# FFN gate and up tiles as block products of seven multiplications, with one operand summed by an accumulating transfer

## The chip, the cores and the metric

One Trainium2 (trn2) chip, one core. The metric is the device time of one execution of the whole program in microseconds (us), the median of several executions. One more execution is profiled; its trace gives the rows shown below.

## The reference

A decoder trunk of two layers over 512 tokens of width 1024, all in float32. Each layer is a token mixer and then a dense SwiGLU FFN; only the FFN is touched here.

```
FF = 2816
def _swiglu(h, w_gate_up, w_down):
    gu = jnp.einsum('bsd,df->bsf', h, w_gate_up)      # 1024 -> 2 x 2816
    g, u = gu[..., :FF], gu[..., FF:]
    return jnp.einsum('bsf,fd->bsd', jax.nn.silu(g) * u, w_down)
...
    hn = _rmsnorm(h, norm_ffn[layer])
    h = h + _swiglu(hn, w_gate_up[layer], w_down[layer])
```

## The kernel before

The activations lie feature by token: a tile is 128 features on the partitions by T = 512 tokens, and the residual x is KC = 8 such tiles. Float32 products are made of three matmuls: each operand is split into a high part (a copy rounded to fp32r, on ScalarE) and a low part (what the copy lost, a subtraction on VectorE), and `mm3` adds high x high, high x low and low x high in PSUM.

`unit` (L58 to L67) brings 128 x 1024 weights: one load on the SP queue into a buffer of `rawp` (three of them), then `whi` on ScalarE and `wlo` on VectorE (pool `wp`, three of each). `feature_tile` makes one tile of 128 outputs by 512 tokens in a PSUM bank of `psg` (four banks) from such a unit and a list of split inputs. Other tiles lie in two pools of 128 x 512 buffers: `low` (33) and `slots` (39); `slot(name, type, low)` picks one. Temporary PSUM banks come from `psa` (four).

`ffn` has NF = 22 pairs of tiles. Each pair is one gate tile and one up tile (L549, L554), both over the eight chunks of the input; the input is x times the norm's weight, and the row factor `rb` (the inverse root mean square of each token) is multiplied in afterwards (L551, L555), since the matmuls start before it is known. Silu and the product follow (L552, L556), and the product is split into `a_h` and `a_l`, the first eight pairs into `low`, the others into `slots`. Then each of the eight output tiles is one PSUM bank over all 22 products, loaded in the three pieces of `DOWN`, and is added to x (L564). `feed` prepares the new x tile for the next layer; in the last layer `final_turn` and `finish` do the final norm and the output, and `finish` makes the last tile in two halves of 256 tokens.

No order is written out for the FFN. The engines' queues are filled by a planner, which picks, for each engine, among the instructions whose operands and buffers are there, by their place in the program; each queue then runs in its order, and semaphores hold an instruction until its operands are ready. `tc.keep_in_program_order` and `tc.issue_after` pin single instructions.

Of the kernel before, what the change touches and what calls it, by code (L numbers as in the profile page):

```python
# [16 lines left out]
F32 = mybir.dt.float32  # L17
# [4 lines left out]
ALU = mybir.AluOpType  # L22
# [12 lines left out]
NEG = -1e30  # L35
ORDER = "S0 A0 B0 C0 S1 T0 U0+A1 V0+B1 C1 S2 T1 U1+A2 V1+B2 C2 S3 T2 U2+A3 V2+B3 C3 -0 T3 U3 V3"
WARM = 8
DOWN = [(0, 8), (8, 15), (15, 22)]


class Trunk:
# [196 lines left out]
    def mixer(self, wf, wt, wsb, wro, wout, tabs, dec):  # L238
# [297 lines left out]
        for i in range(8):  # L536
# [3 lines left out]
                self.start_norm(self.norm_col + 1)  # L540
            self.feed(i)

    def ffn(self, wgu, wdn, last):
        nc, xs, slot = self.nc, self.xs, self.slot
        ax = []
        for f in range(NF):
            g = self.feature_tile(wgu[2 * f], xs)
            if f == 0:
                rb = self.rms_rows(self.acc, D)  # L549
            gs = slot("g")  # L550
            nc.vector.tensor_tensor(out=gs, in0=g, in1=rb, op=ALU.mult)  # L551
            nc.scalar.activation(gs, gs, AF.Silu)  # L552
            u = self.feature_tile(wgu[2 * f + 1], xs)
            us = slot("u")  # L554
            nc.vector.tensor_tensor(out=us, in0=u, in1=rb, op=ALU.mult)  # L555
            nc.vector.tensor_tensor(out=us, in0=us, in1=gs, op=ALU.mult)  # L556
            ax.append(self.split(us, "a", f < 8))
        if last:
            self.tc.keep_in_program_order(nc.scalar.preload_act_table_set("sqrt_and_others"))
        for i in range(KC - 1 if last else KC):  # L560
            ps = self.bank()
            for a, b in DOWN:
                self.feature_tile(wdn[i][:, a * P : b * P], ax[a:b], ps, a == 0, b == NF)
            nc.vector.tensor_tensor(out=self.x[i], in0=self.x[i], in1=ps, op=ALU.add)  # L564
            if i == 0:
                self.start_norm(self.norm_col + 1)
            if last:
                self.square(i)
                self.final_turn(i)
            else:  # L570
                self.feed(i)
        return ax


    def final_turn(self, c, lo=0, hi=T):
# [11 lines left out]
            if c == 3:  # L587
                nc.vector.tensor_copy(self.xt[t][0], ps)

    def finish(self, wdn, ax, out):  # L590

        nc, c = self.nc, KC - 1
        units = [self.unit(wdn[c][:, a * P : b * P], (b - a) * P) for a, b in DOWN]
        for lo in (0, T // 2):
            hi = lo + T // 2
            ps = self.bank()[:, : T // 2]
            for (a, b), u in zip(DOWN, units):
                self.feature_tile(u, [(h[:, lo:hi], l[:, lo:hi]) for h, l in ax[a:b]], ps, a == 0, b == NF)
            x = self.x[c][:, lo:hi]
            nc.vector.tensor_tensor(out=x, in0=x, in1=ps, op=ALU.add)  # L600
            sq = self.slot("sq7")
            nc.scalar.activation(sq[:, lo:hi], x, AF.Square)
            self.final_turn(c, lo, hi)
            ts = range(lo // P, hi // P)
            y = self.rms_tokens([self.acc, sq], D, ts)
            for j, t in enumerate(ts):
                xt, rows = self.xt[t], slice(t * P, (t + 1) * P)
                nc.vector.tensor_scalar(out=xt[0], in0=xt[0], scalar1=y[:, j : j + 1], scalar2=None, op0=ALU.mult)
                nc.scalar.activation(xt[1], self.turned[t], AF.Copy, scale=y[:, j : j + 1])
                nc.sync.dma_start(out=out[rows, 0:T], in_=xt[0])  # L610
                nc.scalar.dma_start(out=out[rows, T:D], in_=xt[1])

    def run(self, xT, norms, tabs, dec, sqr, wq, wf, wt, wsb, wro, wout, wgu, wdn, out):
# [15 lines left out]
        nc.gpsimd.affine_select(out=self.keep, in_=self.keep, pattern=[[-1, T]], base=T - P - 1, channel_multiplier=1, compare_op=ALU.not_equal, fill=0.0)  # L629
        for l in range(L):  # L630
            self.mixer(wf[l], wt[l], wsb[l], wro[l], wout[l], tabs, dec)
            ax = self.ffn(wgu[l], wdn[l], l == L - 1)
        self.finish(wdn[L - 1], ax, out)


@with_exitstack
# [65 lines left out]
```

## Time and profile before

| | |
|---|---|
| median of 3 runs | 1655.45 us (1655.44 to 1655.64) |
| the profiled execution's own time | 1655.86 us |
| its span, from the first instruction to the last | 1653.8 us |
| TensorE busy | 1638.4 us (99%) |
| VectorE busy | 952.7 us (58%) |
| ScalarE busy | 689.0 us (42%) |
| GpSimd busy | 69.6 us (4%) |
| moved by DMA | 153.40 MB, 93 GB/s on average |

PE is TensorE's matmuls, PEld its weight loads, DVE VectorE, ACT ScalarE, POOL GpSimd, SP SyncE, whose queue (SPq) issues the loads. L63 is line 63 of the kernel. Busy time of PE is that of pipelined matmuls, whose ends are modelled, so it is their starts that tell the pace.

### The profile page before, as it was taken

What the parts mean: (1) busy time and instruction counts of PE and PEld (TensorE: products, weight loads), DVE (VectorE), ACT (ScalarE), POOL (GpSimd) and SP (SyncE); (2) the same over time, 40 slices, a digit from 0 to 9 for tenths busy, and PEclk for the clock granted to TensorE, in tenths of its full rate; (3) what the DMA queues carried; (4) which work ended last, traced back from release to release, by engine and by line L of the source; (5) the groups of instructions that cost most, each with busy time, mean ns of one, the idle gap of its engine ahead of it and who ended that gap; (6) DMA issues with size and microseconds to landing.
All of it is one profiled execution on the core that took longest, in us unless ns stands there. A gap on an engine that the chain in (4) does not pass through costs nothing.

```text
span 1653.8 us, 18844 instructions
## 1 busy us (share of the span) xinstructions
PE 1638.4 (99%) x7474; PEld 1341.7 (81%) x7474; DVE 952.7 (58%) x1307; ACT 689.0 (42%) x1053; POOL 69.6 (4%) x57
## 2 busy tenths in 40 slices
PE   9999999999999999999999999999999999999998
PEld 7887777888888888888888778888888888888887
DVE  5799878645554444433348987885354544444232
ACT  5667745433342323222227677453324333233222
POOL 2000000000200000001000000000002000000000
PEclk9999999999999999999999999999999999999999
DMA  5322312233333232333332122223333333333331
GB/s 194 103 76 77 102 53 64 89 102 102 95 97 100 92 102 89 97 94 93 101 100 90 64 90 90 62 70 102 98 100 91 103 91 101 94 97 96 92 95 62
DMA packets 45591, 153.40 MB, mean 93 GB/s; under 512 B 5184, under 2 KB 5696, under 8 KB 45504
## 3 DMA queue, kind: packets, MB, share of 16 engines
q1 hardware_dynamic: 43056, 148.00, 29.0%
q10 hardware_dynamic: 2448, 4.22, 0.8%
q8 instruction: 58, 0.95, 0.2%
q14 instruction: 29, 0.24, 0.0%
HBM read 150.10 MB, written 2.10 MB: 92 GB/s over the span
## 4 chain that ended last, share of the span: by engine, by line
PE 89%; DVE 8%; ACT 2%; issue 1%; DMA 0%; SPq 0%; DVEq 0%; ACTq 0%
PE g L80 26%; PE g L79 26%; PE g L81 26%; PE g L111 2%; PE g L112 2%; PE g L113 2%; DVE wlo L65 2%; DVE z L367 1%; PE a L81 1%; DVE rt L295 1%; PE a L80 1%; PE a L79 1%; DVE kl L341 1%; DVE w L363 1%; ACT whi L63 1%
## 5 line engine op out<-in xcount | busy, mean ns | idle before, releaser
L63 ACT ACTIVATE whi<-raw 128x1024 fp32r<-128x1024 f32 (+1 forms) x276 | 289.1, 1048 | 742.5 <-PE g L80 412.1
L80 PE MATMUL g<-xl,whi 128*128 128x512 f32 x1344 | 524.1, 390 | 0.1
L81 PE MATMUL g<-xh,wlo 128*128 128x512 f32 x1344 | 523.5, 389 | 0.0
L79 PE MATMUL g<-xh,whi 128*128 128x512 f32 x1344 | 521.5, 390 | 0.5 <-ACT xh L169 0.5
L65 DVE TENSOR_TENSOR wlo<-raw,whi 128x1024 fp32r<-128x1024 f32 (+1 forms) x276 | 335.9, 1218 | 162.6 <-ACT whi L63 160.6
L79 PEld LDWEIGHTS g<-xh,whi 128*128 128x128 f32 x1344 | 252.3, 188 | 54.0 <-ACT xh L169 1.4
L80 PEld LDWEIGHTS g<-xl,whi 128*128 128x128 f32 x1344 | 252.3, 188 | 52.4 <-DVE xl L171 0.5
L81 PEld LDWEIGHTS g<-xh,wlo 128*128 128x128 f32 x1344 | 252.3, 188 | 52.3
L80 PE MATMUL g<-a_l,whi 128*128 128x512 f32 (+1 forms) x374 | 142.4, 381 | 0.0
L79 PE MATMUL g<-a_h,whi 128*128 128x512 f32 (+1 forms) x374 | 142.2, 380 | 0.0
L81 PE MATMUL g<-a_h,wlo 128*128 128x512 f32 (+1 forms) x374 | 141.7, 379 | 0.0
L555 DVE TENSOR_TENSOR u<-g,rs_y 128x512 f32<-128x512 f32 x44 | 30.4, 691 | 134.8 <-PE g L81 134.8
L228 POOL TENSOR_TENSOR acc<-acc,sq 128x512 f32<-128x512 f32 x34 | 55.7, 1638 | 1069.0 <-ACT sq L227 1068.5
L79 PEld LDWEIGHTS g<-a_h,whi 128*128 128x128 f32 x374 | 70.1, 187 | 14.8
L551 DVE TENSOR_TENSOR g<-g,rs_y 128x512 f32<-128x512 f32 x44 | 30.4, 691 | 89.3 <-PE g L81 89.3
L80 PEld LDWEIGHTS g<-a_l,whi 128*128 128x128 f32 x374 | 70.1, 187 | 14.3
L81 PEld LDWEIGHTS g<-a_h,wlo 128*128 128x128 f32 x374 | 70.1, 187 | 14.2
L111 PE MATMUL g<-whi,xh 128*128 128x512 f32 x192 | 74.9, 392 | 1.0 <-ACT v L314 1.0
L113 PE MATMUL g<-wlo,xh 128*128 128x512 f32 x192 | 75.0, 391 | 0.0
L112 PE MATMUL g<-whi,xl 128*128 128x512 f32 x192 | 74.9, 390 | 0.0
L367 DVE TENSOR_TENSOR_SCAN z<-keep,w 128x256 f32<-128x256 bf16 (+2 forms) x64 | 51.0, 818 | 1.6
L79 PE MATMUL g<-rt_h,whi 128*128 128x512 f32 x128 | 49.8, 389 | 0.0
(162 smaller groups left out, 1927.1 us busy)
## 6 DMA issues: line engine op xcount, KB each, us to landing
raw<-in_wgu SPq DMA_DIRECT2D x88, 512.0 KB, 3.5
raw<-in_wf SPq DMA_DIRECT2D x76, 512.0 KB, 3.5
raw<-in_wdn SPq DMA_DIRECT2D x32, 448.0 KB, 3.3
raw<-in_wt SPq DMA_DIRECT2D x24, 512.0 KB, 3.6
raw<-in_wro SPq DMA_DIRECT2D x16, 512.0 KB, 3.5
raw<-in_wout SPq DMA_DIRECT2D x16, 512.0 KB, 3.6
raw<-in_wdn SPq DMA_DIRECT2D x16, 512.0 KB, 3.6
raw<-in_wsb SPq DMA_DIRECT2D x8, 512.0 KB, 3.5
```

Source lines behind the costliest of these rows:

```text
L63: self.last_hi = nc.scalar.activation(hi[:, :n], raw[:, :n], AF.Copy).ins
L65: nc.vector.tensor_tensor(out=lo[:, :n], in0=raw[:, :n], in1=hi[:, :n], op=ALU.subtract)
L79: mm(out, lhsT=ah, rhs=bh, start=start, stop=False)
L80: mm(out, lhsT=ah, rhs=bl, start=False, stop=False)
L81: self.last_mm = mm(out, lhsT=al, rhs=bh, start=False, stop=stop).ins
L111: mm(out, lhsT=ah, rhs=bh, start=start, stop=False)
L112: mm(out, lhsT=al, rhs=bh, start=False, stop=False)
L113: mm(out, lhsT=ah, rhs=bl, start=False, stop=stop)
L228: nc.gpsimd.tensor_tensor(out=self.acc, in0=self.acc, in1=sq, op=ALU.add)
L367: nc.vector.tensor_tensor_scan(out=s[:, o:e][:, ::-1], data0=keep[:, ::-1], data1=w[:, o:e][:, ::-1], initial=NEG, op0=ALU.mult, op1=ALU.s ...
L551: nc.vector.tensor_tensor(out=gs, in0=g, in1=rb, op=ALU.mult)
L555: nc.vector.tensor_tensor(out=us, in0=u, in1=rb, op=ALU.mult)
```

## The change

Of the 22 pairs of gate and up tiles in a layer, the first five (`PLAIN`) stay as they are; the other 17 are made by `pair`. It sees the pair as a product of a 2 x 2 block matrix of weights (rows: gate and up; columns: the lower and the upper half of the 1024 inputs) with a 2 x 2 block matrix of inputs (rows: the same halves; columns: tokens 0 to 255 and 256 to 511). Seven block products, with sums of blocks as operands, take the place of eight. With A the weights and B the input, S1 = A21 + A22, S2 = S1 - A11, S3 = A11 - A21 and S4 = A12 - S2 are made for each pair, T1 = B12 - B11, T2 = B22 - T1, T3 = B22 - B12 and T4 = T2 - B21 once a layer by `pair_input`, which needs the row factor first, so that the pairs' results aren't multiplied by it afterwards (the code keeps S2, T2 and T4 with the sign turned). Each block product (`block`) is four chunks of three matmuls with 256 tokens.

Sums of products are made in PSUM where matmuls can go on adding in one bank, and by ScalarE copies and VectorE additions elsewhere. S1 is made by two transfers: the first half of the up tile's weights is loaded into a buffer `s1` once more from DRAM, and a transfer issued by GpSimd adds the second half to it. `pair` is a generator with five pieces, and the loop in `ffn` puts the last two pieces of a pair between the first three of the next.

The down projection is cut into two halves of 11 products each. The first is run after pair 12, the second at the end; each adds all eight output tiles into x. The split of a product into its low part (`low_part`) is moved from the pair to the down projection's first tile, whose matmuls are put in an order of their own. `XLOW`, `ALOW` and `LLOW` say which of the new tiles lie in `low`.

```
@@ -35,7 +35,11 @@
 NEG = -1e30
 ORDER = "S0 A0 B0 C0 S1 T0 U0+A1 V0+B1 C1 S2 T1 U1+A2 V1+B2 C2 S3 T2 U2+A3 V2+B3 C3 -0 T3 U3 V3"
 WARM = 8
-DOWN = [(0, 8), (8, 15), (15, 22)]
+PLAIN = 5
+HALF = NF // 2
+XLOW = 8
+ALOW = 16
+LLOW = False
 class Trunk:
@@ -540,10 +544,124 @@
                 self.start_norm(self.norm_col + 1)
             self.feed(i)
+    def raw_unit(self, src):
+        raw = self.rawp.tile([P, 1024], F32, name="raw", tag="raw")
+        self.nc.sync.dma_start(out=raw, in_=src)
+        return raw
+    def pair_weights(self, gate, up):
+        nc, tt = self.nc, self.nc.vector.tensor_tensor
+        a, b = self.raw_unit(gate), self.raw_unit(up)
+        p, q = slice(0, T), slice(T, 2 * T)
+        s1 = self.slot("s1")
+        def wide(src):
+            hi, lo = self.wp.tile([P, 1024], F32R, name="whi", tag="whi"), self.wp.tile([P, 1024], F32R, name="wlo", tag="wlo")
+            nc.scalar.activation(hi, src, AF.Copy)
+            tt(out=lo, in0=src, in1=hi, op=ALU.subtract)
+            return [(hi[:, s], lo[:, s]) for s in (p, q)]
+        w = {}
+        w["A11"], w["A12"] = wide(a)
+        nc.sync.dma_start(out=s1, in_=up[:, p])
+        nc.gpsimd.dma_start(out=s1, in_=up[:, q], accum_op=ALU.add)
+        w["A22"] = self.split(b[:, q], "w")
+        tt(out=b[:, p], in0=a[:, p], in1=b[:, p], op=ALU.subtract)
+        tt(out=b[:, q], in0=a[:, p], in1=s1, op=ALU.subtract)
+        w["S3"], w["S2"] = wide(b)
+        w["S1"] = self.split(s1, "w")
+        tt(out=a[:, q], in0=a[:, q], in1=b[:, q], op=ALU.add)
+        w["S4"] = self.split(a[:, q], "w")
+        return w
+    def pair_input(self, c, rb):
+        nc, tt = self.nc, self.nc.vector.tensor_tensor
+        h = T // 2
+        p, q = slice(0, h), slice(h, T)
+        b1, b2, u, v = (self.slot(n) for n in ("xn", "xn", "xu", "xv"))
+        for t, k in ((b1, c), (b2, c + 4)):
+            nc.vector.scalar_tensor_tensor(out=t, in0=self.x[k], scalar=self.norms[:, self.norm_col * KC + k : self.norm_col * KC + k + 1], in1=rb, op0=ALU.mult, op1=ALU.mult)
+        tt(out=u[:, p], in0=b1[:, q], in1=b1[:, p], op=ALU.subtract)
+        tt(out=u[:, q], in0=b2[:, q], in1=b1[:, q], op=ALU.subtract)
+        tt(out=v[:, p], in0=u[:, p], in1=b2[:, q], op=ALU.subtract)
+        tt(out=v[:, q], in0=b2[:, p], in1=v[:, p], op=ALU.add)
+        low = lambda: self.xlow.pop() if self.xlow else False
+        if c % 2 == 0:
+            l = low()
+            self.b11 = self.slot("xb_h", F32R, l), self.slot("xb_l", F32R, l)
+        s = slice(c % 2 * h, c % 2 * h + h)
+        hi, lo = (t[:, s] for t in self.b11)
+        nc.scalar.activation(hi, b1[:, p], AF.Copy)
+        tt(out=lo, in0=b1[:, p], in1=hi, op=ALU.subtract)
+        self.xf["B11"].append((hi, lo))
+        for t, names in ((b2, ("B21", "B22")), (u, ("T1", "T3")), (v, ("T2", "T4"))):
+            hi, lo = self.split(t, "xf", low())
+            for name, s in zip(names, (p, q)):
+                self.xf[name].append((hi[:, s], lo[:, s]))
+    def block(self, out, w, x, start):
+        hi, lo = w
+        for c, (xh, xl) in enumerate(self.xf[x]):
+            s = slice(c * P, (c + 1) * P)
+            for k, (l, r) in enumerate(((hi, xh), (lo, xh), (hi, xl))):
+                self.nc.tensor.matmul(out, lhsT=l[:, s], rhs=r, start=start and c == 0 and k == 0, stop=c == 3 and k == 2, skip_group_check=True)
+    def pair(self, wgu, f):
+        nc, tt = self.nc, self.nc.vector.tensor_tensor
+        h = T // 2
+        p, q = slice(0, h), slice(h, T)
+        w = self.pair_weights(wgu[2 * f], wgu[2 * f + 1])
+        x, zy = self.bank(), self.abank()
+        t, u3 = self.slot("pu"), self.slot("u3")
+        self.block(x[:, p], w["A11"], "B11", True)
+        nc.scalar.activation(t[:, p], x[:, p], AF.Copy)
+        self.block(zy[:, p], w["A12"], "B21", True)
+        yield
+        self.block(x[:, p], w["S2"], "T2", False)
+        nc.scalar.activation(t[:, q], x[:, p], AF.Copy)
+        self.block(zy[:, q], w["S1"], "T1", True)
+        yield
+        self.block(x[:, p], w["S3"], "T3", False)
+        nc.scalar.activation(u3[:, p], x[:, p], AF.Copy)
+        tt(out=x[:, q], in0=zy[:, q], in1=u3[:, p], op=ALU.add)
+        yield
+        self.block(x[:, p], w["A22"], "T4", False)
+        yield
+        self.block(zy[:, q], w["S4"], "B22", False)
+        tt(out=t, in0=zy, in1=t, op=ALU.add)
+        nc.scalar.activation(t, t, AF.Silu)
+        self.activated(x, t)
+        yield
+    def activated(self, u, g):
+        a, hi = self.slot("a", F32, self.alow()), self.slot("a_h", F32R, self.alow())
+        self.nc.vector.tensor_tensor(out=a, in0=u, in1=g, op=ALU.mult)
+        self.nc.scalar.activation(hi, a, AF.Copy)
+        self.ax.append((hi, a))
+    def alow(self):
+        self.na += 1
+        return (self.na - 1) % (2 * HALF) >= 2 * HALF - ALOW
+    def low_part(self, f):
+        hi, a = self.ax[f]
+        lo = self.slot("a_l", F32R, LLOW)
+        self.nc.vector.tensor_tensor(out=lo, in0=a, in1=hi, op=ALU.subtract)
+        self.ax[f] = hi, lo
     def ffn(self, wgu, wdn, last):
         nc, xs, slot = self.nc, self.xs, self.slot
-        ax = []
-        for f in range(NF):
+        self.ax, self.na, self.xf, self.xlow = [], 0, {n: [] for n in ("B11", "B21", "B22", "T1", "T2", "T3", "T4")}, XLOW * [True]
+        for f in range(PLAIN):
             g = self.feature_tile(wgu[2 * f], xs)
             if f == 0:
                 rb = self.rms_rows(self.acc, D)
@@ -553,15 +671,60 @@
             u = self.feature_tile(wgu[2 * f + 1], xs)
             us = slot("u")
             nc.vector.tensor_tensor(out=us, in0=u, in1=rb, op=ALU.mult)
-            nc.vector.tensor_tensor(out=us, in0=us, in1=gs, op=ALU.mult)
-            ax.append(self.split(us, "a", f < 8))
+            self.activated(us, gs)
+            if f < 4:
+                self.pair_input(f, rb)
+        old = None
+        for f in range(PLAIN, NF):
+            new = self.pair(wgu, f)
+            next(new)
+            if old:
+                next(old)
+            next(new)
+            if old:
+                next(old)
+            next(new)
+            old = new
+            if f == HALF + 1:
+                self.down(wdn, 0, range(KC))
         if last:
             self.tc.keep_in_program_order(nc.scalar.preload_act_table_set("sqrt_and_others"))
-        for i in range(KC - 1 if last else KC):
+        self.down(wdn, 1, range(KC - 1 if last else KC), old, last)
+    def down(self, wdn, half, tiles, old=None, last=False):
+        nc, f0 = self.nc, half * HALF
+        cuts = [(f0, f0 + 6), (f0 + 6, f0 + HALF)]
+        for i in tiles:
             ps = self.bank()
-            for a, b in DOWN:
-                self.feature_tile(wdn[i][:, a * P : b * P], ax[a:b], ps, a == 0, b == NF)
+            units = [(a, b, self.unit(wdn[i][:, a * P : b * P], (b - a) * P)) for a, b in cuts]
+            if i == 0:
+                mm = nc.tensor.matmul
+                for a, b, (hi, lo) in units:
+                    for f in range(a, b):
+                        if old and f == f0 + 4:
+                            next(old)
+                        if old and f == f0 + 6:
+                            next(old)
+                        if f != f0 + HALF - 1 or not old:
+                            self.low_part(f)
+                    for f in range(a, b):
+                        s = slice((f - a) * P, (f - a + 1) * P)
+                        mm(ps, lhsT=hi[:, s], rhs=self.ax[f][0], start=f == f0, stop=False)
+                        mm(ps, lhsT=lo[:, s], rhs=self.ax[f][0], start=False, stop=False)
+                if old:
+                    self.low_part(f0 + HALF - 1)
+                for a, b, (hi, lo) in units:
+                    for f in range(a, b):
+                        s = slice((f - a) * P, (f - a + 1) * P)
+                        mm(ps, lhsT=hi[:, s], rhs=self.ax[f][1], start=False, stop=f == f0 + HALF - 1)
+            else:
+                for a, b, u in units:
+                    self.feature_tile(u, self.ax[a:b], ps, a == f0, b == f0 + HALF)
             nc.vector.tensor_tensor(out=self.x[i], in0=self.x[i], in1=ps, op=ALU.add)
+            if not half:
+                continue
             if i == 0:
                 self.start_norm(self.norm_col + 1)
             if last:
@@ -569,7 +732,6 @@
                 self.final_turn(i)
             else:
                 self.feed(i)
-        return ax
     def final_turn(self, c, lo=0, hi=T):
@@ -587,15 +749,16 @@
             if c == 3:
                 nc.vector.tensor_copy(self.xt[t][0], ps)
-    def finish(self, wdn, ax, out):
+    def finish(self, wdn, out):
         nc, c = self.nc, KC - 1
-        units = [self.unit(wdn[c][:, a * P : b * P], (b - a) * P) for a, b in DOWN]
+        cuts = [(HALF, HALF + 6), (HALF + 6, NF)]
+        units = [self.unit(wdn[c][:, a * P : b * P], (b - a) * P) for a, b in cuts]
         for lo in (0, T // 2):
             hi = lo + T // 2
             ps = self.bank()[:, : T // 2]
-            for (a, b), u in zip(DOWN, units):
-                self.feature_tile(u, [(h[:, lo:hi], l[:, lo:hi]) for h, l in ax[a:b]], ps, a == 0, b == NF)
+            for (a, b), u in zip(cuts, units):
+                self.feature_tile(u, [(h[:, lo:hi], l[:, lo:hi]) for h, l in self.ax[a:b]], ps, a == HALF, b == NF)
             x = self.x[c][:, lo:hi]
             nc.vector.tensor_tensor(out=x, in0=x, in1=ps, op=ALU.add)
             sq = self.slot("sq7")
@@ -629,8 +792,8 @@
         nc.gpsimd.affine_select(out=self.keep, in_=self.keep, pattern=[[-1, T]], base=T - P - 1, channel_multiplier=1, compare_op=ALU.not_equal, fill=0.0)
         for l in range(L):
             self.mixer(wf[l], wt[l], wsb[l], wro[l], wout[l], tabs, dec)
-            ax = self.ffn(wgu[l], wdn[l], l == L - 1)
-        self.finish(wdn[L - 1], ax, out)
+            self.ffn(wgu[l], wdn[l], l == L - 1)
+        self.finish(wdn[L - 1], out)
 @with_exitstack
```

## Rows read from the trace of the kernel before

**Rows 1.** the page: span, busy time, granted clock of PE in 40 slices

```profile
span 1653.8 us, 18844 instructions
...
PE 1638.4 (99%) x7474; PEld 1341.7 (81%) x7474; DVE 952.7 (58%) x1307; ACT 689.0 (42%) x1053; POOL 69.6 (4%) x57
...
PEclk9999999999999999999999999999999999999999
```

**Rows 2.** the page: the chain that ended last, shares of the span by engine

```profile
PE 89%; DVE 8%; ACT 2%; issue 1%; DMA 0%; SPq 0%; DVEq 0%; ACTq 0%
```

**Rows 3.** busy time by stage: gate and up, then down, of layer 0

```profile
core 0: us, PE busy (x) PEld busy (x) DVE busy (x) ACT busy (x) POOL busy (x), PEclk, DMA share, GB/s
470.70:701.00 230.30, 230.30 (x1018) 190.70 (x1017) 110.22 (x133) 71.70 (x89) 0.00 (x0) 1.00 0.32 97
701.00:823.50 122.50, 122.50 (x532) 99.24 (x531) 38.91 (x42) 33.46 (x40) 9.34 (x6) 1.00 0.33 96
```

**Rows 4.** line L551, gate tiles' first multiplication, window 487 to 697 us

```profile
L551 DVE TENSOR_TENSOR g<-g,rs_y x20: 691/691/692, 489.2 to 695.9; 128x512 f32<-128x512 f32 x20
```

**Rows 5.** timeline of PE, last tile: start us, us, engine, line, operation

```profile
1628.03 0.28 PE L79 MATMUL g<-a_h,whi 128*128 128x256 f32 x1
...
1630.06 0.28 PE L81 MATMUL g<-a_h,wlo 128*128 128x256 f32 x1
...
1632.10 0.28 PE L81 MATMUL g<-a_h,wlo 128*128 128x256 f32 x1
...
1634.93 0.28 PE L79 MATMUL g<-a_h,whi 128*128 128x256 f32 x1
```

**Rows 6.** timeline of all engines, same place: two weight loads

```profile
1628.14 0.19 PEld L81 LDWEIGHTS g<-a_h,wlo 128*128 128x128 f32 x1
...
1628.26 0.19 PEld L79 LDWEIGHTS g<-a_h,whi 128*128 128x128 f32 x1
```

**Rows 7.** groups by shape, DVE: count | busy us, mean ns of one | idle before

```profile
L65 DVE TENSOR_TENSOR wlo<-raw,whi 128x1024 fp32r<-128x1024 f32 x244 | 300.9, 1235 | 111.3 <-ACT whi L63 110.8
...
L555 DVE TENSOR_TENSOR u<-g,rs_y 128x512 f32<-128x512 f32 x44 | 30.4, 691 | 134.8 <-PE g L81 134.8
L234 DVE TENSOR_TENSOR a_l<-u,a_h 128x512 fp32r<-128x512 f32 x44 | 30.2, 685 | 1.4 <-ACT a_h L233 1.4
...
L600 DVE TENSOR_TENSOR x<-x,g 128x256 f32<-128x256 f32 x2 | 0.8, 420 | 11.3 <-PE g L81 11.3
```

**Rows 8.** groups by shape, ACT, same columns

```profile
L63 ACT ACTIVATE whi<-raw 128x1024 fp32r<-128x1024 f32 x244 | 258.6, 1060 | 620.2 <-issue 305.9 <-PE g L80 289.8 <-PE g L112 19.5
...
L233 ACT ACTIVATE a_h<-u 128x512 fp32r<-128x512 f32 x44 | 27.8, 632 | 28.7 <-DVE u L556 28.7
...
L602 ACT ACTIVATE sq<-x 128x256 f32<-128x256 f32 x2 | 0.8, 416 | 11.6 <-DVE x L600 11.6
```

**Rows 9.** timeline of all engines, gate and up: a buffer released, loaded, copied

```profile
501.01 1.22 DVE L65 TENSOR_TENSOR wlo<-raw,whi 128x1024 fp32r<-128x1024 f32 x1 [0.22 <-ACT whi L63]
...
502.26 6.25 SPq L61 DMA_DIRECT2D raw<-in_wgu  x2
...
505.36 1.06 ACT L63 ACTIVATE whi<-raw 128x1024 fp32r<-128x1024 f32 x1 [3.86 <-issue]
```

**Rows 10.** line L559, the table load for Sqrt

```profile
L559 ACT ACT_TABLE_LOAD  x1: 1283/1283/1283, 1521.6 to 1521.6; - x1
```

**Rows 11.** DMA issues: count, KB each, median us from issue to landing

```profile
raw<-in_wgu SPq DMA_DIRECT2D x88, 512.0 KB, 3.5
...
x<-in_xT SPq DMA_DIRECT2D x8, 256.0 KB, 5.3
...
cosr<-in_tabs ACTq DMA_DIRECT2D x2, 256.0 KB, 2.7
```

**Rows 12.** timeline of DVE, gate and up of layer 0

```profile
490.13 1.22 DVE L65 TENSOR_TENSOR wlo<-raw,whi 128x1024 fp32r<-128x1024 f32 x1 [0.22 <-ACT whi L63]
494.66 0.69 DVE L555 TENSOR_TENSOR u<-g,rs_y 128x512 f32<-128x512 f32 x1 [3.30 <-PE g L81]
```

## The prediction

> **What bounds the kernel now.** I read the page first. TensorE (PE) is busy for 1638.4 of 1653.8 us at a granted clock of 9 tenths or more in all 40 slices [rows 1], and the chain that ended last is PE for 89% [rows 2]. A busy PE alone proves little, since its matmuls are pipelined, so I went on to the table by stage. The gate-and-up stage of layer 0 runs from 470.7 to 701 us without an idle moment of PE, VectorE (DVE) busy 110.2 of its 230.3 us and ScalarE (ACT) 71.7; the down stage is the same with DVE at 38.9 of 122.5 [rows 3]. The reader is to see that in both stages everything but PE has room: a stage costs its matmul columns times their pace. The pace is read from the multiplication by the row norm that follows each gate tile: 20 of them between 489.2 and 695.9 us, so 206.7 / 19 = 10.88 us for a pair of gate and up tiles, 48 matmuls of 512 columns, 226.7 ns each [rows 4].
>
> **What the change removes on PE.** A pair of plain tiles is 2 x 8 x 3 = 48 matmuls of 512 columns. A pair by seven products is 7 blocks x 4 chunks x 3 = 84 matmuls of 256 columns: 7/8 of the columns, but 84 weight loads in place of 48. What it is worth hangs on the pace of a 256-column matmul with a load of its own. The last output tile of the kernel is made of just these. Its first 18, whose moving tile lies in the pool `low`, start between 1628.03 and 1630.06: 2.03 / 17 = 119.4 ns. A later stretch, whose moving tile lies in `slots`, has 26 starts from 1632.10 to 1634.93: 2.83 / 25 = 113.2 ns [rows 5]. These are my bounds: 84 x 113.2 = 9.51 us, or 84 x 119.4 = 10.03 us, against 10.88. In the new code the first eight splits of the transformed input go to `low`: 48 of a pair's 84 matmuls read them, 36 read `slots`. Taken so, a pair is 48 x 0.1194 + 36 x 0.1132 = 9.81 us. There are 17 such pairs in each of 2 layers: 34 x (10.88 - 9.81) = **36.4 us saved** (46.6 at one bound, 28.9 at the other).
>
> The weight loads might speak against this. Each load is shown as 0.19 us long, but two in the 256-column stretch start 0.12 us apart [rows 6]: they overlap one another and the matmuls, so 84 of them fit in 9.81 us. The Trainium skill says otherwise where it tells how to judge TensorE (Perfetto Trace Analysis, "Identifying the Most-Contended Engine"): the share of time in weight loads, not in matmuls, is the measure. By that measure the change would raise the load from 48 to 84 a pair and be a loss; I keep it as a rival below, and the trace does not agree with reading it as a bound.
>
> **What it adds on DVE and ACT.** From the rows of instructions of the same size [rows 7, 8], DVE does, per pair: two wide low parts 2 x 1.235, three 512-column low parts 3 x 0.685, three sums over weights 3 x 0.69, one 256-column sum 0.42, the gate's sum and the product 2 x 0.69: 8.4 us of 9.81, 86%. ACT: two wide copies 2 x 1.06, three narrow 3 x 0.63, three 256-column copies out of PSUM 3 x 0.42, Silu and the high part of the product 2 x 0.63: 6.5 us. Both are below PE's 9.81, so throughput does not bound the stage; order and latency may:
>
> - *PSUM.* The next block into the same bank must wait until ACT has copied the last partial sum out (0.42), in one place until DVE has added after that (0.42). The loop puts two blocks of other banks between, 24 x 0.117 = 2.8 us. Only with a wide copy ahead on ACT (1.06) and a wide low part ahead on DVE (1.24) is it late, 3.14 against 2.8. Bounds 0 and 34 x 0.34 = 11.6 us; most handovers meet at most one of the two, so I take 0.1 each: **+3.4**.
> - *Weights ahead of PE.* Three raw buffers serve two loads a pair, and each is now held until its sums are made. From the release of a raw buffer to the next high-part copy takes 505.36 - 502.23 = 3.13 us [rows 9]. Then: the subtraction 0.69 (beside the first ACT copy), the low part of A22 0.69, the second subtraction 0.69, ACT's wide copy 1.06, the wide low part 1.24, the low part of S4 0.69: 8.2 us round the ring, if the other 4.4 us of DVE work go into the 3.13 + 1.06 us in which this chain waits for others. They just do; hidden behind PE's 9.81, **0**, with 1.6 us of slack. Not hidden it is the second rival.
> - *The plain tiles.* Beside four of the five plain pairs DVE also builds the seven input blocks, 2 x 0.69 + 5 x 0.42 + 3 x 0.685 = 5.5 us on top of 2 x 1.235 + 3 x 0.69 = 4.5: 10.1 of 10.88. Bounds 0 and one wide low part late in each of 8 pairs, 9.9; nearer to none, since PE's weights are made ahead: **+1**.
>
> **The down projection** keeps its matmul count; it is cut into two halves, so each output tile is added into x twice. That, and the low parts moved there (11 x 0.685 = 7.5 us a half), lies on a DVE that is busy a third of that stage [rows 3]: 0; without that cover, 16 extra additions of 0.69 would cost 11. At the start of the second half the last pair is unfinished: after its last block come sum, Silu, product and high part, 0.69 + 0.63 + 0.69 + 0.63 = 2.6 us, while about 8 matmuls of 0.23 cover 1.9. Bounds 0 and 2.6 + 0.69 a layer; **+3** for both. In layer 1 the table for Sqrt is loaded ahead of that Silu, so the tables may be loaded twice more, 1.28 us each [rows 10], one of them perhaps near the end: **+1** (0 to 2.6).
>
> **The transfer that adds.** No accumulating transfer is in the trace. A plain load of 256 KB takes 2.7 to 5.3 us to land [rows 11]; the one that adds comes after it, so S1 is there 5.4 to 10.6 us after its first issue. It needs no raw buffer, only a slot, so it can start about a pair early, and the queues are not kept in the program's order: the wide low part at 490.13 us is of a later tile than the one whose result DVE takes at 494.66, since PE was already at work on that [rows 12]. I take 0; its upper end is the fourth rival. The Trainium skill (DMA: Bandwidth & Descriptors, "Anatomy of one DMA") gives some 2.0 us and the bytes at 436 GB/s for a transfer issued by GpSimd, an estimate of 2.6 us here, which no row shows.
>
> **The sum**, against the profiled execution's own 1655.86 us (span 1653.8, 2.1 around it): 1655.86 - 36.4 + 3.4 + 1 + 3 + 1 = 1627.9; the median of the runs is 0.4 below the profiled one: **1627.5 us**.
>
> **Rivals.**
> 1. *Forecast*, pairs at PE's pace with small waits: 1627.5, by itself 1611 (all at 113.2 ns, 2 us of waits) to 1645 (all at 119.4, the waits at their upper bounds in part). Chance 0.62.
> 2. *The raw ring sets the pace.* If the results out of PSUM (0.42 + 0.69 + 0.69) hold DVE just when the ring needs it, and the ring's 8.2 us become 8.2 + 1.8 + 0.4 = 10.4, a pair costs 10.4: 34 x 0.48 = 16.3 saved, 1655.9 - 16.3 + 8.4 = 1648. For it: DVE at 86%. Against: the slack of 1.6 us. Chance 0.16.
> 3. *Weight loads one after another.* 84 x 0.19 = 16.0 us a pair [rows 6], 34 x 5.1 = +174: about 1830. Against it stand rows 5 and 6. Chance 0.02.
> 4. *Slower: the adding transfer is late.* If the first load of S1 queues on SP behind a raw load that waits for its buffer, the ring closes through both transfers: with 3.5 and 4.4 us (between the plain loads of 3.5 and 5.3) 7.9, then subtraction, wide copy, wide low part and the low part of S4, 0.69 + 1.06 + 1.24 + 0.69 = 3.7: 11.6 us. 34 x 0.72 + 8.4 = +33: 1688. It decides from two transfers of 6.9 us together, where a pair costs 10.6 and the waits eat the rest. For it: nothing in the code gives S1 priority. Against: rows 12. Chance 0.14.
> 5. *Neither.* The waits sum to the gain, between 1652 and 1659: 0.06.
>
> **How the numbers follow.** A difference of 0.2%, 3.3 us, is about what a measurement of this kernel can tell. Faster: all of 1, nearly all of 2 (0.15): 0.77. Same: most of 5, 0.05. Slower: 4, 3 and what is left of 2 and 5: 0.18. The range takes case 1 whole from 1609 and most of 2, and ends at 1660, which leaves out case 4, case 3 and little more.
>
> **What would show it.** Right: in the gate-and-up stage the products `a` come 9.5 to 10.1 us apart, PE has no idle time there, 256-column matmuls start 113 to 120 ns apart, and DVE is near 85%. Case 2: PE waits for `wlo` or `whi` in each pair. Case 4: PE and DVE wait on a chain that ends in the transfer into `s1`. Wrong altogether: a 256-column pace outside 113 to 120 ns with weights taken from `slots`, which no stretch of the last tile shows, or a wait at every block for a copy out of PSUM.

## The result, and the profile after

The changed kernel takes 1765.81 us (median of 4 runs, 1764.86 to 1766.51), the kernel before 1655.55 us beside it (4 runs): a ratio of 1.0664, 95% interval 1.0651 to 1.0677. That is slower, where 1627.5 us was forecast, and outside the range. It went the way of the fourth rival, and further: that rival gave 1688. The profiled execution took 1765.38 us, 109.5 more than the profiled one of before.

The page of the changed kernel, its span, busy times, granted clock (PEclk: tenths of full speed, in 40 slices of the span) and the two transfers of `s1` (its tile is named `s`):

```profile
span 1763.6 us, 21961 instructions
...
PE 1666.3 (94%) x8665; PEld 1405.5 (80%) x8665; DVE 1119.1 (63%) x1623; ACT 796.9 (45%) x1307; POOL 97.6 (6%) x91
...
PEclk9999999999999899999999999999999999999999
...
s<-in_wgu SPq DMA_DIRECT2D x34, 256.0 KB, 4.6
s<-in_wgu POOLq DMA_DIRECT2D x34, 256.0 KB, 4.2
```

PE was busy for 99% of the span [rows 1], now for 94%. No other engine is near its limit. So something makes PE wait. The windows of the changed kernel, first over the stretch that rows 3 show of before (it now holds a part of the first down projection too), then four short ones around one wait, and the line of the product `a` (L647) in part of that stretch. The columns are those of rows 3:

```profile
470.70:701.00 230.30, 211.62 (x1206) 186.10 (x1205) 136.64 (x201) 87.31 (x139) 8.78 (x10) 0.95 0.37 106
```

```profile
583.00:591.40 8.40, 8.39 (x70) 8.19 (x68) 2.90 (x4) 1.30 (x4) 0.86 (x1) 0.98 0.55 158
591.40:594.30 2.90, 0.26 (x3) 0.05 (x1) 1.25 (x2) 0.63 (x2) 0.00 (x0) 0.87 0.43 72
594.30:600.40 6.10, 5.89 (x26) 5.60 (x27) 4.90 (x8) 3.83 (x6) 0.00 (x0) 0.50 0.36 103
600.40:606.00 5.60, 5.59 (x47) 5.39 (x47) 1.81 (x3) 1.29 (x3) 0.86 (x1) 1.00 0.49 139
```

```profile
L647 DVE TENSOR_TENSOR a<-g,pu x5: 683/684/685, 551.9 to 611.4; 128x512 f32<-128x512 f32 x5
```

The products are (611.4 - 551.9) / 4 = 14.9 us apart, where a pair took 10.88 [rows 4]. PE stands still for most of 591.4 to 594.3 and then runs at a granted clock of 0.50, the 1.2 GHz level, for some 6 us. Who keeps it waiting is in the waits (engine, line, tile, what it waited for: us in total, times, longest), first the engines', then those of the load queue:

```profile
POOL s L572 <- DMA s<-in_wgu: 258.2, 10, 60.9
...
ACT w_h L237 <- DMA s<-in_wgu: 142.1, 28, 6.0
...
PE a L614 <- ACT w_h L237: 50.5, 29, 2.7
...
PE a L614 <- DVE w_l L238: 15.9, 32, 1.9
```

```profile
SPq L552 <- DVE wlo L566: 317.8, 28, 18.9
...
SPq L552 <- DVE w_l L238: 30.2, 26, 5.9
```

ScalarE stands for 142 us before its copy of `s` (S1's high part), until the adding transfer lands, and PE stands behind ScalarE. In the pairs the load queue's largest wait is at a raw load (L552), for the wide low part that frees one raw buffer; the next waits, for less, for the low part of S4 (`w_l`), which frees another. The first transfer of `s1` (L571) has no wait of its own in that answer: it goes out when the raw loads ahead of it have gone. One turn, from the timeline (start, length, engine, line, operation; idle time before it and what ended that in brackets):

```profile
581.77 1.53 SPq L552 DMA_DIRECT2D raw<-in_wgu  x2
...
582.26 0.68 DVE L238 TENSOR_TENSOR w_l<-raw,w_h 128x512 fp32r<-128x512 f32 x1
...
583.65 0.33 SPq L571 DMA_DIRECT2D s<-in_wgu  x1
...
589.37 0.86 POOL L572 DMA_DIRECT2D s<-in_wgu  x1 [14.42 <-DMA s<-in_wgu]
...
593.67 0.63 ACT L237 ACTIVATE w_h<-s 128x512 fp32r<-128x512 f32 x1 [6.02 <-DMA s<-in_wgu]
593.74 0.69 DVE L575 TENSOR_TENSOR raw<-raw,s 128x512 f32<-128x512 f32 x1 [1.35 <-DMA s<-in_wgu]
...
594.72 1.99 ACT L565 ACTIVATE whi<-raw 128x1024 fp32r<-128x1024 f32 x2
...
595.80 1.23 DVE L566 TENSOR_TENSOR wlo<-raw,whi 128x1024 fp32r<-128x1024 f32 x1 [0.16 <-ACT whi L565]
```

The second of the two raw loads of the first row, and the first one of the next turn:

```profile
582.97 0.33 SPq L552 DMA_DIRECT2D raw<-in_wgu  x1
```

```profile
597.05 0.33 SPq L552 DMA_DIRECT2D raw<-in_wgu  x1
```

This is the ring of rival 4. A raw buffer comes free at 581.77, and this pair's up tile is asked for; the next pair's gate tile follows at 582.97, when the low part of S4 has freed its buffer. Only then, 1.88 us after the first, goes the first transfer of `s1`. GpSimd asks for the adding one 5.72 us after that, when the first has landed, and 4.30 us later ScalarE can copy. Then follow subtraction (L575), wide copy, wide low part, 3.38 us in all, and at 597.05 the buffer is free again: 1.88 + 5.72 + 4.30 + 3.38 = 15.28 us. PE at the same place, its matmuls of 256 columns:

```profile
589.82 0.28 PE L614 MATMUL g<-xf_h,w_l 128*128 128x256 f32 x1
...
591.38 0.28 PE L614 MATMUL a<-xf_l,w_h 128*128 128x256 f32 x1
594.35 0.58 PE L614 MATMUL a<-xf_h,w_h 128*128 128x256 f32 x1 [2.69 <-ACT w_h L237]
595.09 0.58 PE L614 MATMUL a<-xf_h,w_l 128*128 128x256 f32 x1 [0.16 <-DVE w_l L238]
...
595.68 0.41 PE L614 MATMUL a<-xf_h,w_h 128*128 128x256 f32 x1
...
597.39 0.41 PE L614 MATMUL a<-xf_l,w_h 128*128 128x256 f32 x1
```

Before the wait 13 steps from start to start take 1.56 us (589.82 to 591.38), 120 ns each. After it 8 steps take 1.71 us (595.68 to 597.39), 214 ns each, at 1.2 GHz.

**The account.** I sum the times from each start of a pair's matmul to PE's next start over the whole trace: 474.5 us for 34 pairs, 13.96 us a pair. Starts that follow at once, at the full clock, are 118.2 ns apart, so 84 of them are 9.93 us, which is the floor of a pair. Gaps over that come to 116 us; 233 matmuls at 1.2 GHz, in 18 stretches, cost 21.5 us more; together that is 4.0 us a pair. Against 10.88 before, 34 x 3.08 = +104.7 us; the other 4.8 of the 109.5 lie outside the pairs.

### The profile page after: what moved, and what is told of

Its sections match the earlier page's. It is cut to its first block, busy times and chain, and to the rows that moved or that the text cites. A ratio compares the mean times of both kernels' runs of the same rounds, so it can differ in the third digit from the quotient of the medians.

```text
span 1763.6 us, 21961 instructions
## 1 busy us (share of the span) xinstructions
PE 1666.3 (94%) x8665; PEld 1405.5 (80%) x8665; DVE 1119.1 (63%) x1623; ACT 796.9 (45%) x1307; POOL 97.6 (6%) x91
## 5 line engine op out<-in xcount | busy, mean ns | idle before, releaser
L84 PE MATMUL g<-xl,whi 128*128 128x512 f32 x800 | 312.6, 391 | 0.3 <-DVE xl L175 0.3
L85 PE MATMUL g<-xh,wlo 128*128 128x512 f32 x800 | 311.9, 390 | 0.0
L83 PE MATMUL g<-xh,whi 128*128 128x512 f32 x800 | 310.5, 392 | 0.4 <-ACT xh L173 0.4
L83 PEld LDWEIGHTS g<-xh,whi 128*128 128x128 f32 x800 | 150.5, 188 | 32.7 <-ACT xh L173 1.6
L84 PEld LDWEIGHTS g<-xl,whi 128*128 128x128 f32 x800 | 150.4, 188 | 31.5 <-DVE xl L175 0.6
L85 PEld LDWEIGHTS g<-xh,wlo 128*128 128x128 f32 x800 | 150.4, 188 | 31.2
L614 PE MATMUL a<-xf_h,w_h 128*128 128x256 f32 x272 | 85.0, 312 | 50.5 <-ACT w_h L237 50.5
L614 PE MATMUL a<-xf_h,w_l 128*128 128x256 f32 x272 | 86.6, 319 | 15.9 <-DVE w_l L238 15.9
L614 PE MATMUL g<-xf_h,whi 128*128 128x256 f32 x272 | 85.6, 315 | 4.4 <-ACT pu L625 3.5
L614 PE MATMUL a<-xf_l,w_h 128*128 128x256 f32 x272 | 83.1, 307 | 0.0
```

What stands on the lines that cost most here:

```text
L83: mm(out, lhsT=ah, rhs=bh, start=start, stop=False)
L84: mm(out, lhsT=ah, rhs=bl, start=False, stop=False)
L85: self.last_mm = mm(out, lhsT=al, rhs=bh, start=False, stop=stop).ins
L614: self.nc.tensor.matmul(out, lhsT=l[:, s], rhs=r, start=start and c == 0 and k == 0, stop=c == 3 and k == 2, skip_group_check=True)
```

## The experiments

Each run stands beside the kernel before on its own chip. "Per pair" is the sum just described divided by 34, and "PE waits" is the part of it, in us, that lies in gaps over the floor and not in matmuls at 1.2 GHz. Both come from the profiled execution.

| kernel | S1's halves summed by | us | before | per pair | PE waits |
|---|---|---|---|---|---|
| the change | adding transfer | 1765.81 (4 runs) | 1655.55 | 13.96 | 116 |
| s1_first | the same, asked for ahead of the raw loads | 1764.25 | 1655.67 | 13.94 | 116 |
| act_queue | the same, first transfer on ScalarE's queue | 1847.15 | 1655.67 | 16.42 | 167 |
| own_buffer | the same, `s1` with a buffer of its own | 1669.28 | 1656.18 | 11.14 | 42 |
| s1_ahead | the same, asked for a pair earlier | 1644.24 | 1656.18 | 10.41 | 17 |
| s1_ahead_timed | the same kernel again | 1650.59 (5 runs) | 1655.97 | 10.67 | 25 |
| no_add | first transfer alone | 1637.91 | 1655.67 | 10.30 | 14 |
| dve_sum | VectorE | 1653.11 | 1655.67 | 10.70 | 27 |
| raw4_dve_sum | VectorE, four raw buffers | 1650.41 | 1656.18 | 10.69 | 27 |
| pool_sum | GpSimd | 1641.11 | 1656.18 | 10.39 | 16 |
| pool_sum_timed | the same kernel again | 1642.09 (4 runs) | 1655.97 | 10.41 | 17 |
| pool_sum_s4 | GpSimd, which makes S4 too | 1663.31 (4 runs) | 1655.97 | 11.04 | 39 |
| ahead_pool_bp | a pair earlier; gate - up on GpSimd | 1637.24 | 1655.97 | 10.24 | 11 |
| ahead_bp_timed | the same kernel again | 1637.05 (4 runs) | 1655.83 | 10.19 | 9 |
| ahead_bp_no_add | first transfer alone, a pair earlier | 1635.02 | 1655.83 | 10.19 | 9 |

Where no number of runs is given it is one. The change, s1_first and act_queue have pair matmuls at 1.2 GHz; the others have none.

**s1_first: the requests written ahead of the pair's raw loads.**

```
         s1 = self.slot("s1")
+        nc.sync.dma_start(out=s1, in_=up[:, p])
+        nc.gpsimd.dma_start(out=s1, in_=up[:, q], accum_op=ALU.add)
+        a, b = self.raw_unit(gate), self.raw_unit(up)
```

> Both transfers into s1 are put ahead of the two raw loads of their pair in the program, so that the first one no longer queues on SP behind a raw load that waits for its buffer. Theory A (the ring of raw buffers closes through both transfers, since s1 is issued behind the raw load): s1 is complete before the raw tiles are, the ring falls from some 14.5 us to 8.2 to 10.4 us, a pair costs about 10 us, the kernel about 1630 us (1620 to 1655). Theory B (three raw buffers, or VectorE with its queue, are too slow for a pair whatever s1 does): at least 1740 us. Theory C (a transfer that adds, issued by GpSimd, is slow or blocked in itself): no better than 1740 us, with ScalarE still waiting for s1.

13.94 us a pair: nothing changed. In the SP queue the first transfer of a pair still stands behind three raw loads, its own two and the next pair's first. Its place among the pair's loads in the program was not what put it there, so the theory as first stated fell, and what was left was its buffer, or how early in the whole order it is asked for.

**act_queue: the first transfer on another queue.**

```
-        nc.sync.dma_start(out=s1, in_=up[:, p])
+        nc.scalar.dma_start(out=s1, in_=up[:, p])
```

> Only the queue of the first transfer into s1 is changed: ScalarE issues it in place of SP, the adding transfer stays. It no longer stands behind a waiting raw load, but may stand behind ScalarE's copies. Theory A: much of the loss goes, 1630 to 1690 us. Theory B: 1755 to 1775 us, no change. Theory C: 1740 us or more.

It got worse, far outside theory A's range. Off SP's queue the transfer lands in 2.6 us (median), not 4.6, but the request now stands among ScalarE's copies, one of them the copy that waits for the pair before's adding transfer. Two waits of this run:

```profile
ACT w_h L237 <- DMA s<-in_wgu: 118.2, 32, 6.9
...
PE a L614 <- ACT w_h L237: 106.9, 32, 3.9
```

A faster landing bought nothing, since the request was late. The waits also set the clock back more often: 583 pair matmuls in 32 stretches at 1.2 GHz, 54.6 us more.

**own_buffer: `s1` in a buffer that nothing else uses.**

```
-        self.slots = pool("slots", 39)
+        self.slots = pool("slots", 38)
...
-        s1 = self.slot("s1")
+        s1 = self.sm.tile([P, T], F32, name="s1", tag="s1", bufs=1)
```

> The program is that of the change, but s1 gets one buffer of its own and the pool slots has 38 instead of 39. In the SP queue of the change s1 of a pair stands behind three raw loads (its own two and the next pair's first); with a buffer of its own the planner puts it behind its own first raw load alone, nearly a pair earlier. Theory A2 (what is late is the first transfer into s1, and it is late because no buffer of slots is free when the planner wants to place it): s1 is complete when the raw tiles are, a pair costs 9.9 to 10.5 us, the kernel 1632 to 1650 us. Theory C (a transfer that adds is slow or blocked in itself): 1740 us or more, ScalarE still waits for s1.

1669.28 us is slower than theory A2 had it and far faster than theory C. 2.82 us a pair come back by the buffer alone, and in the SP queue the transfer now stands behind one raw load of its pair, not three loads. So the shared pool `slots` was part of what held it back. What is left is a ring through the one buffer:

```profile
565.97 0.33 SPq L571 DMA_DIRECT2D s<-in_wgu  x1
...
567.72 2.06 SPq L552 DMA_DIRECT2D raw<-in_wgu  x2
...
569.05 0.86 POOL L572 DMA_DIRECT2D s<-in_wgu  x1 [10.69 <-DVE wlo L566]
...
575.95 0.63 ACT L237 ACTIVATE w_h<-s 128x512 fp32r<-128x512 f32 x1 [1.66 <-DMA s<-in_wgu]
...
577.34 0.33 SPq L571 DMA_DIRECT2D s<-in_wgu  x1
```

The adding transfer runs beside two raw loads of 512 KB, and it takes 6.9 us until ScalarE can copy (the median landing of this run is 6.5 us, against 4.2 in the change, where none of the 34 met a raw load). The buffer is free 11.37 us after its first request, and the SP queue now stands at that request, with the raw loads behind it:

```profile
SPq L571 <- DMA s<-in_wgu: 126.1, 21, 6.4
```

**s1_ahead: `s1` asked for a pair earlier**, in a buffer of `slots` again.

```
+    def pair_sum(self, up):
+        s1 = self.slot("s1")
+        self.nc.sync.dma_start(out=s1, in_=up[:, :T])
+        self.nc.gpsimd.dma_start(out=s1, in_=up[:, T:], accum_op=ALU.add)
+        self.sums.append(s1)
...
-        s1 = self.slot("s1")
+        s1 = self.sums.pop(0)
...
+        self.pair_sum(wgu[2 * PLAIN + 1])
         for f in range(PLAIN, NF):
+            if f < NF - 1:
+                self.pair_sum(wgu[2 * f + 3])
```

> Both transfers into s1 are asked for one pair earlier in the program, in a buffer of slots as before. In the SP queue it stands behind one raw load of its pair, as in own_buffer. Theory A2: 1632 to 1655 us, perhaps with a few us of waits for the slots that s1 now holds longer. Theory C: 1740 us or more.

> The program of s1_ahead, timed in rounds against the kernel before: 1644 us, a ratio of 0.992 to 0.995 with all of its interval below 1.

10.41 us a pair and 1644.24 us, then 1650.59 in the timed runs (1647.83 to 1654.33), a ratio of 0.9963 (0.9948 to 0.9977): a gain, but less than the 0.992 to 0.995 expected. The 10.67 us a pair in the table are those of the slowest of the five. ScalarE no longer waits for `s` at all. The same two transfers by the same queues, given a lead, turn the loss into a gain.

**no_add: the adding transfer left out** (S1 is then only half made).

```
         nc.sync.dma_start(out=s1, in_=up[:, p])
-        nc.gpsimd.dma_start(out=s1, in_=up[:, q], accum_op=ALU.add)
```

> The adding transfer is left out (s1 then holds the first half of the up tile alone), the first one stays where it was on SP. Theory A: the ring loses the 0.6 us of hand-over and 4.3 us of the adding transfer, 14.5 to some 9.7 us: about 1635 us (1622 to 1665). Theory B: 1740 us or more. Theory C: as A, so that s1_first tells A from C.

10.30 us a pair: in the program's own place the adding transfer costs 3.66 us a pair, 124 us in all. The first transfer, still behind its raw loads, costs little: kernels without any transfer (below) take 10.39 and more. Theories A and C both allow this result; s1_ahead, with the same adding transfer, is what rules out C.

**dve_sum and raw4_dve_sum: no transfer; VectorE adds the two halves that the raw buffer holds.** The second has four raw buffers (37 slots).

```
-        nc.sync.dma_start(out=s1, in_=up[:, p])
-        nc.gpsimd.dma_start(out=s1, in_=up[:, q], accum_op=ALU.add)
+        tt(out=s1, in0=b[:, p], in1=b[:, q], op=ALU.add)
```

> No transfers into s1 at all: VectorE adds the two halves of the raw up tile (one more 128x512 sum of 0.69 us a pair). Theory A: the ring is 8.2 + 0.7 us or a little more, VectorE at 9.1 us of 9.8; about 1635 us (1622 to 1660). Theory B: at least 1740 us, and worse than the change by VectorE's extra 23 us. Theory C: as A.

> dve_sum with four raw buffers instead of three and 37 buffers of slots instead of 39. If the ring of raw buffers holds dve_sum back: pairs near 10.0 us, 1628 to 1640 us. If VectorE does, by its amount of work and its order: within 5 us of dve_sum's 1653. If slots are short: slower than dve_sum.

10.70 us a pair, and 10.69 with a fourth raw buffer: with the transfers gone the pairs cost more than the forecast's 9.81 and than rival 2's 10.4, and a raw buffer more gives nothing, so it doesn't look like the raw ring that holds them (that run also has two slots fewer, and no run tells the two apart). What PE's weight loads wait for in dve_sum, and a window inside the pairs of layer 0 (columns as in rows 3):

```profile
PEld a L613 <- DVE w_l L238: 9.4, 30, 1.6
PEld g L613 <- ACT pu L628: 7.5, 32, 0.4
...
PEld g L613 <- DVE wlo L566: 3.4, 6, 1.2
```

```profile
525.00:600.00 75.00, 74.85 (x596) 71.28 (x595) 57.68 (x84) 39.69 (x69) 0.00 (x0) 1.00 0.33 100
```

VectorE's low parts come late most, in short waits, though VectorE is busy for 57.68 of 75 us only; then the copies out of PSUM, 0.2 us in nearly every pair.

**pool_sum: GpSimd adds the halves.**

```
-        nc.sync.dma_start(out=s1, in_=up[:, p])
-        nc.gpsimd.dma_start(out=s1, in_=up[:, q], accum_op=ALU.add)
+        nc.gpsimd.tensor_tensor(out=s1, in0=b[:, p], in1=b[:, q], op=ALU.add)
```

> No transfers into s1: GpSimd adds the two halves of the raw up tile (a 128x512 sum, 1.3 to 1.6 us on GpSimd in the rows of before). Takes VectorE's extra 0.7 us out of dve_sum and the transfers out of the change. If dve_sum is held back by VectorE (pairs at 10.70 us): 1635 to 1645 us. If by the ring of raw buffers (the sum lies in the ring in both): 1650 to 1665 us.

> The program of pool_sum, timed in rounds: 1641 us, a ratio of 0.990 to 0.992. If the transfers beside the raw loads cost anything of their own once they are early, pool_sum is below s1_ahead by 2 us or more in every round.

1642.09 us (1641.33 to 1642.31), a ratio of 0.9915 (0.990 to 0.993), though one such sum takes GpSimd 1.32 us (median) against VectorE's 0.69. Taking one sum a pair off VectorE is worth 0.3 us a pair.

VectorE has the same work here as in s1_ahead, and every run is over 5 us below the fastest of s1_ahead_timed. By the expectation above, transfers beside the raw loads do cost something there, however early they are. The row that differs is VectorE's wait for the up tile's raw load: in s1_ahead_timed it comes to 50.0 us (the row stands further down), in dve_sum, without transfers, to 4.9, and in pool_sum GpSimd stands there in VectorE's place. The row of dve_sum:

```profile
DVE s L571 <- DMA raw<-in_wgu: 4.9, 7, 1.6
```

**pool_sum_s4: the sum for S4 on GpSimd as well.**

```
-        tt(out=a[:, q], in0=a[:, q], in1=b[:, q], op=ALU.add)
+        nc.gpsimd.tensor_tensor(out=a[:, q], in0=a[:, q], in1=b[:, q], op=ALU.add)
```

> pool_sum with one more 128x512 sum moved from VectorE to GpSimd, the one that S4 is split from (0.69 us a pair less on VectorE, 1.3 to 2.2 us on GpSimd). The pairs of pool_sum take 10.39 us where 84 matmuls take 9.93. If what is left is VectorE's load: 10.1 to 10.2 us a pair, 1632 to 1638 us. If it is the handing over in PSUM, through ScalarE's queue: 1639 to 1643 us. If the sum on GpSimd is now late for S4 or holds the raw buffers: above 1645 us.

1663.31 us, slower than the kernel before by a little (1.0044, 1.0029 to 1.0059) and than pool_sum by 21 us. The sum for S4 is the last link of its chain, and the slower engine makes it late. Two waits of this run:

```profile
ACT w_h L237 <- POOL raw L577: 27.9, 34, 4.0
...
PE g L613 <- ACT pu L624: 21.4, 28, 0.8
```

In each pair ScalarE stands at S4's copy until GpSimd is done; behind it in ScalarE's queue are the copies out of PSUM (L624) that PE waits for.

**ahead_pool_bp: `s1` a pair earlier, and the subtraction gate - up on GpSimd.**

```
-        tt(out=b[:, p], in0=a[:, p], in1=b[:, p], op=ALU.subtract)
+        nc.gpsimd.tensor_tensor(out=b[:, p], in0=a[:, p], in1=b[:, p], op=ALU.subtract)
```

> s1_ahead with the first subtraction (gate minus up, for S3) moved from VectorE to GpSimd, beside its adding transfers. If VectorE's load holds s1_ahead at 10.41 us a pair: 1634 to 1641 us. If the handing over in PSUM does: 1642 to 1646 us. If GpSimd's queue now delays the adding transfers: above 1650 us.

> Timed: the halves of the up tile summed by the adding transfer, asked for a pair earlier, and the gate-minus-up subtraction on GpSimd. Theory A (the transfer costs only its lateness; given a pair's lead it is free, and what is left is VectorE's order): 1637 to 1645 us, as in the single look at 1637.24, 10.2 to 10.5 us per pair, at least as fast as the sum made by GpSimd (1642.09). Rival (the single look was a lucky order of transfers; the adding transfer still comes late in some executions, as the same idea without the moved subtraction gave 1644 in one job and 1650 in another): 1645 us or more, or runs spread over more than 3 us.

1637.05 us, a ratio of 0.9891 (0.9875 to 0.9908): the fastest of those that make S1 whole, with 9 us of PE waits in 34 pairs. The four runs go from 1636.27 to 1640.94, a spread of 4.7 us where the rival was given more than 3; but the slowest of them is still below every run of pool_sum_timed. Its page, and what PE still waits for:

```profile
span 1635.7 us, 22052 instructions
...
PE 1614.0 (99%) x8665; PEld 1372.9 (84%) x8665; DVE 1103.3 (67%) x1589; ACT 796.1 (49%) x1307; POOL 144.2 (9%) x125
...
PEclk9999999999999999999999999999999999999999
```

```profile
PE g L618 <- DVE wlo L572: 1.9, 2, 0.9
...
PE g L618 <- ACT pu L629: 0.7, 4, 0.2
PE a L618 <- DVE w_l L238: 0.7, 2, 0.3
```

What moved with the subtraction is a wait for the up tile's raw load. In s1_ahead_timed VectorE itself stood there, with all its other work behind; now GpSimd does. The two lines, of s1_ahead_timed and then of ahead_bp_timed:

```profile
DVE raw L578 <- DMA raw<-in_wgu: 50.0, 25, 4.4
```

```profile
POOL raw L578 <- DMA raw<-in_wgu: 277.9, 25, 43.4
```

The edit also takes 0.69 us a pair of work off VectorE, and no run tells the two effects apart.

**ahead_bp_no_add: the same without the adding transfer** (S1 is half made).

```
-        self.nc.gpsimd.dma_start(out=s1, in_=up[:, T:], accum_op=ALU.add)
```

> The same kernel without the second, adding transfer: s1 then holds the first half of the up tile alone, so the sums made from it are not the reference's. It prices what the early adding transfer still costs. Theory A (nothing is left of it): 10.2 to 10.3 us per pair and 1635 to 1638 us, the same as with it. Rival (it still delays): 10.0 us per pair or less, under 1632 us.

10.19 us a pair with it and without it. Asked for a pair ahead, and with GpSimd at the fresh raw load, the adding transfer costs the pairs nothing, against 3.66 us in its own place. The first transfer is in both kernels, so this doesn't price it. The 2.3 us between the two totals arise outside the pairs, 1.9 of them in the down projection of layer 0; this kernel was run once.

## Why the prediction was wrong

**The step that failed** is "The transfer that adds": "It needs no raw buffer, only a slot, so it can start about a pair early ... I take 0." It did not start early. Its first transfer stood in the SP queue behind three raw loads, the last two of which waited for the wide low part and for S4's low part of the pair before, and both of these waited, through the second subtraction, for that pair's transfers. The upper end of that step, 10.6 us for the two transfers, was nearly what came (5.72 + 4.30 = 10.0), and it belonged on the path. That its lateness is the cause is shown from two sides: leaving the transfer out gives 3.66 us a pair back, and asking for it a pair earlier gives 3.55 (s1_ahead) and 3.29 (the slowest run of s1_ahead_timed). What is left, 0.1 to 0.4 us, goes with VectorE's wait for raw loads; where GpSimd stands there (ahead_bp_timed), the adding transfer costs the pairs nothing. That the pool `slots` is part of why it came late is shown by own_buffer. How the planner weighed the slot against the raw loads stays open, as the traces show queues and not its choices.

I read rows 12 as evidence that queues leave the program's order when something else is ready. They do show that, but a free slot was not a thing that rows 12 show, and the change adds `pu`, `u3`, the transformed input and the products to that pool. The rows could not bear a chance of only 0.14.

**Rival 4** named the place and the ring rightly and was priced too low, at 11.6 us a pair against 13.96 over all pairs. Of the 3.7 us between it and the 15.28 of the turn shown, 2.1 are the two transfers (10.0, not 7.9), 0.4 the subtraction, the wide copy and the wide low part (3.4, not 3.0), and 1.2 the way from there to the issue of `s1` (1.9 us, with a second raw load, where the rival had 0.7 for S4's low part alone). Many turns are shorter than that one. Nor did it count the clock, 21.5 us.

**TensorE's pace** was right: 118.2 ns a matmul inside 113 to 120, 9.93 us a pair, forecast 9.81. That makes the saving 34 x 0.95 = 32.3 us instead of 36.4. The third rival is out: 84 weight loads of 0.19 us would be 16.0 us a pair, and ahead_bp_timed makes a pair in 10.19. The Trainium skill (Perfetto Trace Analysis, "Identifying the Most-Contended Engine") gives the busy share of weight loads, beside the share of peak, as a measure of how close TensorE is to its limit. That a larger share means a loss was my reading and does not stand there: the share rose from 81% [rows 1] to 84% in ahead_bp_timed, which is the faster kernel.

**PSUM, raw ring, VectorE.** I took 3.4 us of waits for PSUM, 0.1 a pair, and 0 for the ring, though the 4.4 us of VectorE's work that were to hide in 3.13 + 1.06 = 4.19 did not quite fit. Without the transfers (dve_sum) PE waits 27 us. 7.5 of them stand at its weight loads for copies out of PSUM, 0.23 in nearly every pair; a fourth raw buffer leaves the 27 as they are, and one sum moved to GpSimd makes them 16 to 17. VectorE's throughput did not bind (57.68 of 75 us, 77%, with a sum more than the 86% was worked out for). The term mis-sized was order: low parts late behind other work of VectorE, which is rival 2's load without its ring. The 27 us, where 3.4 were forecast, take nearly all of the gain: dve_sum is 2.6 us below 1655.67, in one run.

**The rest** (plain tiles, down projection, tables) was put at 5 us. The change shows 4.8 outside the pairs, and ahead_bp_timed 4.4: 1637.36 - 1656.47 + 34 x 0.69, with the profiled executions of that chip. As a sum that was right. ahead_bp_timed, with the transfers early and one subtraction on GpSimd, comes nearest to what was forecast: its 1637.05 us are 9.5 above 1627.5, some 4 for TensorE's pace and 5 to 6 for PE's waits (9 us, not 3.4).

## What to carry to other kernels

A transfer that needs no engine still needs a place in a queue and a buffer: before costing it at nothing, read which loads stand ahead of it, what those wait for, and whether that wait leads back to the transfer. If it does, ask for it one turn of the loop earlier, and time that version before giving the idea up: here the same instructions were 6.6% slower or 0.4% faster, by when they were asked for, and 1.1% faster with one subtraction moved to GpSimd besides. When an engine's queue stops at an operation on a fresh load, that operation is a candidate for an idle engine (one such move gained here, though part of the gain may be VectorE's lighter load); one at the end of a chain is not.

## What the runs showed of the hardware

- The clock. In the pairs of the change PE stands still for over 1 us 32 times, for 2.7 at most, and 18 stretches of the pairs show the 1.2 GHz level: after the 2.69 us shown, matmuls of 256 columns came 214 ns apart for about 6 us. own_buffer, with 42 us of waits in the pairs of which none was over 1.1, kept 9 tenths or more in all 40 slices. A wait can so cost more than its own length.
- A transfer of 256 KB that adds into SBUF, issued by GpSimd, landed after 4.2 us (median of 34) in the change and after 6.5 (median) in own_buffer, where it ran beside loads of 512 KB; in the change none of the 34 did. The estimate of 2.6 us that the prediction worked out from the Trainium skill (DMA: Bandwidth & Descriptors, "Anatomy of one DMA") does not agree with either.
- GpSimd was busy 0.86 us with each issue of such a transfer, and took 1.32 us for a sum of 128 x 512 for which VectorE took 0.69.
